# A two-layer encoder's opening: the small columns' load moved behind the modulation weights, and one modulation sum moved to GpSimd

## The chip, the cores and the metric

The kernel runs on one core of a Trainium2 chip. The metric is the device time of one execution in microseconds (us), taken as the median of several runs. A profiled execution has a span (first to last instruction) and a time of its own, a little longer.

## The reference, cut to what matters

Each of two layers modulates its normed input with vectors that come out of a matrix product with one row, `silu(c) @ adaln_w`. The first layer's first two vectors, shift (`v` = 0) and scale (`v` = 1), are needed before any product of the layer can be finished.

```python
mod = jnp.einsum('bd,lde->lbe', jax.nn.silu(c), adaln_w) + adaln_b[:, None, :]
...
    sh1, sc1, g1, sh2, sc2, g2 = jnp.split(mod[layer][:, None, :].astype(x.dtype), 6, axis=-1)
    h = rmsnorm(x, norm_w[layer, 0]) * (1.0 + sc1) + sh1
    y = hybrid_mixer(h, ...)          # proj = h @ w_in, then three branches
...
    x = x + g1 * rmsnorm(y, norm_w[layer, 1])
    h = rmsnorm(x, norm_w[layer, 2]) * (1.0 + sc2) + sh2
    y = swiglu(h, ...) if layer % 2 == 0 else moe_swiglu(h, ...)
    x = x + g2 * rmsnorm(y, norm_w[layer, 3])
```

There are 256 tokens of width 1024, all in float32.

## The kernel before

Every product is made with weights that are split into a rounded high part (`H`, by ScalarE, L319) and a rest (`L`, by VectorE, L320), and the activations likewise into `xH` and `xL`; three matmuls replace one. Weights arrive as tiles of 128 x 1024 float32, 512 KB each, on the DMA queue that SyncE issues (SP). They stand in one list, `plan`; `load_ahead` issues the load of the next entries, `issue_one` splits the next entry, and `take` hands it to the matmuls. Four `raw` buffers hold loaded weights in turn. A load into a buffer waits until the split of its last user is done. SP issues in order, and each load also waits for the load that stands eight places ahead of it in the queue.

The change lies in `begin`, the opening of layer 0, in which TensorE, VectorE and ScalarE run in the order in which the code is written. A modulation vector has 1024 columns in two halves of 512; half 0 serves the first four 128-blocks of the model width, half 1 the last four. For each half and each of the two vectors, four tiles `rawe` (256 of the 1024 rows each, 512 KB) are loaded, and `adaln_add` multiplies them by the column `scol` and sums them into `acc` on VectorE, two instructions a tile (L450 first, then L452). TensorE then sums over the partitions with one-column matmuls (`ad`, L492), in `end`; `bias` adds `adaln_b`. Some tiles go to TensorE straight away instead (the flag `pe`).

With half 0 done, the first halves of `xH` and `xL` exist, and TensorE can multiply with rows 0 to 511 of the weights: `gv` (two tiles, rows 0 to 511, products `pn`), the small columns (48 columns of `w_in`, loaded by two DMAs of many short rows, L814 and L815, products `pg`) and `nk` (two tiles, products `pt`). With half 1 done, the rows 512 to 1023 follow: `gv` from its other two tiles, the rest of the small columns, the rest of `nk`. From there on the list of weights goes on (`nq`, `nv`, ...), and the order is the same before and after.

`gv` is planned first, then the small columns, then `nk`; a permutation of the first seven entries (in `plan_mixer`) sets the order of their loads. `between` is called after each of the first eight modulation tiles, and spreads the loads of `x` and of small rows and the first norm over them. `G` is GpSimd, `V` VectorE, `S` ScalarE.

Of the kernel before, what the change touches and what calls it, by code (L numbers as in the profile page):

```python
# [77 lines left out]
def _build(ctx, tc, nc, A, out, dbg, upto):  # L78
# [121 lines left out]
    def other_loads():  # L200

        nc.sync.dma_start(cc[:, P:], A["consts"][:, P:])
        nc.sync.dma_start(posi, A["positions"].rearrange("b (t p) -> p (b t)", p=P))
        nc.sync.dma_start(gdnA.rearrange("p l e -> p (l e)"), ap(A["gdn_A_log"], 0, [[0, P], [1, 16]]))
        nc.sync.dma_start(gdnB.rearrange("p l e -> p (l e)"), ap(A["gdn_dt_bias"], 0, [[0, P], [1, 16]]))
# [141 lines left out]
    def issue_one(lows=None):  # L347
        nm_, k0, load, early = plan.popleft()
        r = loaded.popleft() if loaded else load()
        ready.append((nm_, k0) + split(r, early, lows) + (early,))  # L350
# [8 lines left out]
    def load_ahead(tags):  # L359

        for tag in tags:
            t = tl("raw1", [P, 1024], tag) if tag else None
            ahead.append(t)
            loaded.append(plan[len(loaded)][2](t))
# [14 lines left out]
    def take(name, ahead=True):  # L379
        if ahead or not any(r[0] == name for r in ready):  # L380
            issue(ahead, name)
        r = next(r for r in ready if r[0] == name)
        ready.remove(r)
        _, k0, H, L, _ = r
        return [(k0 + i, H[:, i, :], L[:, i, :]) for i in range(H.shape[1])]
# [10 lines left out]
    def mm_nat(o, k, H, L, xs, tb, last, parts=(0, 1)):  # L396

        xH, xL = xs
        if 0 in parts:
            mm(o, xH[:, tb, k, :], H, start=k == 0, stop=False)  # L400
            mm(o, xH[:, tb, k, :], L, start=False, stop=False)  # L401
        if 1 in parts:
            mm(o, xL[:, tb, k, :], H, start=False, stop=k == last)  # L403
# [38 lines left out]
        return o if rows < KD else [t.rearrange("p c t n -> p c (t n)") for t in o]  # L442


    def adaln_add(r, k0, acc, first=0):

        for j in range(r.shape[1]):
            k = k0 + j
            if k == first:
                ts(acc, r[:, j, :], scol[:, k:k + 1], None, op0=OP.mult)  # L450
            else:
                stt(acc, r[:, j, :], scol[:, k:k + 1], acc, op0=OP.mult, op1=OP.add)  # L452

# [32 lines left out]
    def sums(half):  # L486

        o = ps("ad", [P, 2, 4])
        accs, begun = {}, []

        def into(v, j, r, c, last):
            mm(o[:, v, j:j + 1], r[:, j * P:j * P + P], c, start=not begun, stop=last, skip_group_check=True)  # L492
            begun.append(1)

        def add(v, k0, r, pe):
            if pe:
                for k in range(2):
                    for j in range(4):
                        into(v, j, r[:, k], scol[:, k0 + k:k0 + k + 1], False)
            else:  # L500
                first = None
                if v not in accs:
                    accs[v], first = tl("acc", [P, 512], ("la2", "m2")[v]), k0
                adaln_add(r, k0, accs[v], first)

        def end(v=None):
            for u in list(accs) if v is None else [v]:
                acc = accs.pop(u)
                for j in range(4):
                    into(u, j, acc, one_c, v is None and j == 3 and not accs)  # L510

        def bias():
            h = slice(half * 4, half * 4 + 4)
            tt(modT[:, 0, 0:2, h], o, adb[:, 0, 0:2, h], op=OP.add)

        return Steps(add=add, end=end, bias=bias)

    def begin(xs, n, part):


        load = lambda v, half, k0: adaln_load(0, v, half, k0, tl("rawe", [P, 1024], "l4"))
        s0 = sums(0)
        for i in range(8):
            v, k0 = (1, 0)[i % 2], i // 2 * 2
            s0.add(v, k0, load(v, 0, k0), i in (1, 3))
            part(i)
        load_ahead([None] * 2)
        order = [(1, 0), (1, 2), (1, 4), (1, 6), (0, 0), (0, 2), (0, 4), (0, 6)]
        late = [load(v, 1, k0) for v, k0 in order[:2]]
        load_ahead([None, None, "l4"])  # L530
        late += [load(v, 1, k0) for v, k0 in order[2:]]
        lows = []
        s0.end()
        issue_one()
        issue_one(lows)
        s0.bias()
        n.scale(slice(0, 4))
        n.hf(0, 0)
        n.hi(0, 0)
        n.lo(0, 0)  # L540
        lows.pop()()
        n.hf(1, 0, 0)
        n.hi(1, 0)
        n.lo(1, 0)
        load_ahead([None] * 2)
        o = [ps("pn", [P, 512], "pw") for _ in range(2)]

        def product(early, tb, i):
            for k, H, L in early:
                mm_nat(o[tb], k, H, L, xs, tb, KD - 1, (i,))  # L550

        s1 = sums(1)
        late = [(v, k0, r, i == 0) for i, ((v, k0), r) in enumerate(zip(order, late))]
        s1.add(*late[0])
        early = [p for _ in range(2) for p in take("gv", False)]
        for tb in range(2):
            for i in range(2):
                product(early, tb, i)
        issue_one()
        s1.add(*late[1])  # L560
        small = take("small", False)
        osm = gates_small(xs, small[:4])
        issue_one()
        load_ahead([None] * 2)
        other_loads()
        s1.add(*late[2])
        issue_one()
        s1.add(*late[3])
        s1.end(1)
        n.tr(0, 1, ("pg",))  # L570
        n.tr(1, 1, ("pl",))
        onk = proj_T("nk", 512, xs, rows=2)
        for i in range(4, 8):
            s1.add(*late[i])
        issue_one(lows)
        issue_one(lows)
        s1.end()
        proj_T("nk", 512, xs, 1, onk, 2, 4)
        lows.pop(0)()
        s1.bias()  # L580
        n.scale(slice(4, 8))
        n.hf(0, 1, 4)
        n.hf(1, 1, 0)
        n.hi(0, 1)
        lows.pop()()
        n.lo(0, 1)
        early = [p for _ in range(2) for p in take("gv", False)]
        n.hi(1, 1)
        n.lo(1, 1)
        for tb in range(2):  # L590
            for i in range(2):
                product(early, tb, i)
        return o, osm, small[4:], onk

    def row_of(col, name):

# [221 lines left out]
    def gates_small(xs, some=None, o=None):  # L818

        xH, xL = xs  # L820
        o = o or ps("pg", [P, 2, P], "pg" if some else "pl")
        for k, H, L in some or take("small"):
            mm(o[:80], H, xH[:, :, k, :], start=k == 0, stop=False)
            mm(o[:80], L, xH[:, :, k, :], start=False, stop=False)
            mm(o[:80], H, xL[:, :, k, :], start=False, stop=k == KD - 1)
        if k < KD - 1:
            return o
        pump()

        wd = tl("wd", [80, T], "l1")  # L830
        S.copy(wd, o[:80].rearrange("p t n -> p (t n)"))
        G.memset(wd[32:33], 1.0)
        return wd
# [500 lines left out]
    def plan_mixer(l):  # L1334
        w = A["w_in"][l]
        for b in BLOCKS:
            if b == "small":
                plan.append((b, 0, lambda t=None: load_small(w, t), "g4" if l == 0 else None))
            elif b == "out":
                add(b, lambda k0, kn: kview(A["w_out"][l], 0, D, k0, kn), KD, D,  # L1340
                    spare=None if l else "l4")
            elif b[0] == "b":
                n, hf = int(b[1]), int(b[2])
                add(b, lambda k0, kn, n=n, hf=hf: kview(A["w_branch"][l, n], hf * 512, 512, k0, kn), 4, 512)
            else:
                c0 = COL["mg"] + int(b[2]) * D + int(b[3]) * 512 if b[:2] == "mg" else COL[b]
                add(b, lambda k0, kn, c0=c0: kview(w, c0, 512, k0, kn), KD, 512, 4 if b == "gv" else 0, back=6)
        if l == 0:

            first = [plan.popleft() for _ in range(7)]  # L1350
            plan.extendleft(reversed([first[i] for i in (0, 1, 4, 5, 6, 2, 3)]))

    def mixer(l, xs, o, more, then=(), begun=(None, None, None)):
        v = tl("gv", [P, 2, 512], "l4")
# [677 lines left out]

    def between(i):
        n = norm[1]
        for j in ((2,), (3,), (0,), (1, 4, 5, 6), (), (7,), (), ())[i]:
            load_rows(j)
        if i in (0, 1):
            for h in range(2):
                n.sq(i, h)
        elif i == 2:  # L2040
            n.rs(0)
            n.rs(1)
        elif i in (3, 4):
            n.xn(i - 3, 0)
        elif i in (5, 6):
            n.tr(i - 5, 0, ("pg", "pw"))
            columns(i - 5)

    def params():
        columns(2)  # L2050
# [59 lines left out]
```

## Time and profile before

| | |
|---|---|
| median of 3 runs | 1883.06 us (1881.93 to 1888.7) |
| profiled execution, its own time | 1880.3 us |
| its span | 1878.5 us |
| TensorE busy (share of the span) | 1825.1 us (97%) |
| VectorE busy | 1593.7 us (85%) |
| ScalarE busy | 1320.0 us (70%) |
| GpSimd busy | 28.0 us (1%) |
| HBM read | 528.02 MB, 282 GB/s over the span |

Times in the text are microseconds from the span's start. The change moves instructions in the first 60 us or so of 1878.5. Busy time of TensorE counts a matmul until its modelled end, so a busy TensorE can still run at half rate; the distance between the starts of two matmuls tells that.

### The profile page before, as it was taken

How to read it: one execution, taken by the hardware profiler on the slowest of the kernel's cores; microseconds unless marked ns; L12 is line 12 of the kernel's file. 1: busy time of each engine (PE TensorE's matmuls, PEld its weight loads, DVE VectorE, ACT ScalarE, POOL GpSimd, SP SyncE). 2: the span in 40 equal slices, each digit the busy share in tenths (PEclk: the TensorE clock that was granted, in tenths of full speed). 3: DMA queues.
4: the chain of work that ended last, by engine and by line, in shares of the span. 5: the costliest groups of instructions: out<-in, count | busy, mean ns of one | idle time of the engine just before them, and what ended most of it. 6: DMA issues, size and time to landing. Idle time of an engine off the chain costs nothing.

```text
span 1878.5 us, 33240 instructions
## 1 busy us (share of the span) xinstructions
PE 1825.1 (97%) x11984; PEld 1538.5 (82%) x11984; DVE 1593.7 (85%) x2034; ACT 1320.0 (70%) x1872; POOL 28.0 (1%) x54
## 2 busy tenths in 40 slices
PE   7999999999989999999999999999999999999997
PEld 6987888799878977788788888888888888878785
DVE  6887977777766887877798998999989999999998
ACT  3786476643445783576688788787887888888885
POOL 0000000000000000000000000000000000000000
PEclk9999999999999999999999999999999999999998
DMA  9545766478883546758899999999999999999993
GB/s 318 164 143 159 226 191 191 150 250 265 274 278 114 161 140 191 227 161 318 274 364 315 344 349 344 360 374 369 367 336 364 379 368 379 391 385 394 393 392 150
DMA packets 258026, 531.35 MB, mean 283 GB/s; under 512 B 22126, under 2 KB 45116, under 8 KB 257852
## 3 DMA queue, kind: packets, MB, share of 16 engines
q1 hardware_dynamic: 257500, 528.99, 81.1%
q8 instruction: 96, 1.57, 0.4%
q14 instruction: 78, 0.64, 0.1%
q0 software_dynamic: 192, 0.07, 0.0%
q10 hardware_dynamic: 160, 0.07, 0.0%
HBM read 528.02 MB, written 1.05 MB: 282 GB/s over the span
## 4 chain that ended last, share of the span: by engine, by line
PE 72%; DVE 10%; DMA 9%; ACT 5%; issue 3%; POOL 0%; SPq 0%; DVEq 0%; ACTq 0%; POOLq 0%
PE mo L1974 10%; PE mo L1973 10%; PE mo L1975 10%; DVE wl L320 5%; DMA raw<-in_adaln_w 4%; PE pn L400 4%; PE pn L403 3%; PE my L1898 3%; PE my L1899 3%; PE my L1900 3%; PE pn L401 3%; DMA raw<-in_ffn_w 2%; ACT wh L319 2%; PE pt L439 2%; PE pt L440 2%
## 5 line engine op out<-in xcount | busy, mean ns | idle before, releaser
L320 DVE TENSOR_TENSOR wl<-raw,wh 128x1024 fp32r<-128x1024 f32 (+1 forms) x893 | 1067.5, 1221 | 141.0 <-ACT wh L319 110.1
L319 ACT CAST wh<-raw 128x1024 fp32r<-128x1024 f32 (+1 forms) x893 | 927.4, 1054 | 339.9 <-DMA raw<-in_ffn_w 79.1
L1973 PE MATMUL mo<-wh,gx 128*128 128x512 f32 x896 | 356.3, 398 | 0.1
L1974 PE MATMUL mo<-wl,gx 128*128 128x512 f32 x896 | 351.0, 392 | 2.0 <-DVE wl L320 1.9
L1975 PE MATMUL mo<-wh,gx 128*128 128x512 f32 x896 | 350.4, 391 | 0.0
L1974 PEld LDWEIGHTS mo<-wl,gx 128*128 128x128 f32 x896 | 168.8, 188 | 38.9 <-DVE wl L320 5.5
L1975 PEld LDWEIGHTS mo<-wh,gx 128*128 128x128 f32 x896 | 168.5, 188 | 35.8 <-ACT gx L1869 0.4
L1973 PEld LDWEIGHTS mo<-wh,gx 128*128 128x128 f32 x896 | 168.7, 188 | 32.7 <-ACT gx L1869 0.5
L440 PE MATMUL pt<-xH,wl 128*128 128x256 f32 x576 | 164.0, 285 | 3.5 <-DVE wl L320 3.5
L439 PE MATMUL pt<-xH,wh 128*128 128x256 f32 x576 | 166.3, 289 | 0.5 <-ACT wh L319 0.5
L441 PE MATMUL pt<-xL,wh 128*128 128x256 f32 x576 | 163.6, 284 | 0.0
L400 PE MATMUL pn<-wh,xH 128*128 128x512 f32 x352 | 148.6, 422 | 0.0
L403 PE MATMUL pn<-wh,xL 128*128 128x512 f32 x352 | 138.6, 394 | 0.0
L401 PE MATMUL pn<-wl,xH 128*128 128x512 f32 x352 | 138.5, 393 | 0.0
L452 DVE SCALAR_TENSOR_TENSOR acc<-raw,scol,acc 128x512 f32<-128x512 f32 x140 | 104.7, 748 | 28.8 <-DMA raw<-in_adaln_w 27.2
L440 PEld LDWEIGHTS pt<-xH,wl 128*128 128x128 f32 x576 | 111.0, 193 | 4.6 <-DVE wl L320 4.3
L439 PEld LDWEIGHTS pt<-xH,wh 128*128 128x128 f32 x576 | 110.9, 193 | 1.0 <-ACT wh L319 0.7
L441 PEld LDWEIGHTS pt<-xL,wh 128*128 128x128 f32 x576 | 111.0, 193 | 0.0
L1898 PE MATMUL my<-wh,aTm 128*128 128x512 f32 x280 | 109.1, 390 | 0.0
L1899 PE MATMUL my<-wl,aTm 128*128 128x512 f32 x280 | 109.0, 389 | 0.0
L1900 PE MATMUL my<-wh,aTm 128*128 128x512 f32 x280 | 108.9, 389 | 0.0
L400 PEld LDWEIGHTS pn<-wh,xH 128*128 128x128 f32 x352 | 66.5, 189 | 19.0 <-issue 7.4
(474 smaller groups left out, 2605.2 us busy)
## 6 DMA issues: line engine op xcount, KB each, us to landing
raw<-in_moe_w SPq DMA_DIRECT2D x672, 512.0 KB, 5.8
raw<-in_w_in SPq DMA_DIRECT2D x128, 512.0 KB, 3.9
raw<-in_adaln_w SPq DMA_DIRECT2D x80, 512.0 KB, 4.7
raw<-in_ffn_w SPq DMA_DIRECT2D x66, 512.0 KB, 4.7
raw<-in_w_branch SPq DMA_DIRECT2D x24, 512.0 KB, 4.3
rawe<-in_adaln_w SPq DMA_DIRECT2D x16, 512.0 KB, 7.9
raw<-in_w_out SPq DMA_DIRECT2D x16, 512.0 KB, 4.7
x<-in_x SPq DMA_DIRECT2D x2, 512.0 KB, 6.9
```

Source lines behind the costliest of these rows:

```text
L319: S.copy(H, r)
L320: low = lambda: tt(L, r, H, op=OP.subtract)
L400: mm(o, xH[:, tb, k, :], H, start=k == 0, stop=False)
L401: mm(o, xH[:, tb, k, :], L, start=False, stop=False)
L403: mm(o, xL[:, tb, k, :], H, start=False, stop=k == last)
L439: mm(d, H[:, cs], xH[:, :, k, :], start=k == 0 and c % 2 == 0, stop=False, skip_group_check=True)
L440: mm(d, L[:, cs], xH[:, :, k, :], start=False, stop=False, skip_group_check=True)
L441: mm(d, H[:, cs], xL[:, :, k, :], start=False, stop=k == KD - 1, skip_group_check=True)
L1898: mm(y[hf], aT[:, 0, k, :], H[:, c], start=first, stop=False)
L1973: mm(q, gH[:, k, :], H, start=k == 0, stop=False)
L1974: mm(q, gH[:, k, :], L, start=False, stop=False)
L1975: mm(q, gL[:, k, :], H, start=False, stop=k == KD - 1)
```

## The change

The second halves' eight tiles are all loaded right behind the first two `gv` tiles, alternating between the vectors. The small columns' load goes behind the other `gv` tiles, and all of the small columns' product moves behind `gv`'s. The scale vector's second half is summed on GpSimd (a multiply in place and an add, where VectorE has one instruction), the shift vector's on VectorE, none on TensorE. Of the first `gv` products, the second token block's is made behind the second halves' sums. Two extra matmuls (`keep_warm`) stand around the end of the first sums. `between` loads the second block of `x` three places later.

```diff
-    def adaln_add(r, k0, acc, first=0):
+    def adaln_add(r, k0, acc, first=0, eng=V):
...
             if k == first:
-                ts(acc, r[:, j, :], scol[:, k:k + 1], None, op0=OP.mult)
+                eng.tensor_scalar(acc, r[:, j, :], scol[:, k:k + 1], None, op0=OP.mult)
+            elif eng is G:
+                G.tensor_scalar(r[:, j, :], r[:, j, :], scol[:, k:k + 1], None, op0=OP.mult)
+                G.tensor_tensor(acc, r[:, j, :], acc, op=OP.add)
             else:
                 stt(acc, r[:, j, :], scol[:, k:k + 1], acc, op0=OP.mult, op1=OP.add)
...
-                adaln_add(r, k0, accs[v], first)
+                adaln_add(r, k0, accs[v], first, G if v == half == 1 else V)
...
+    def keep_warm():
+
+        mm(ps("warm", [P, 512], "pw"), ident, x[:, 0, 0:512], start=True, stop=True)
...
         load_ahead([None] * 2)
-        order = [(1, 0), (1, 2), (1, 4), (1, 6), (0, 0), (0, 2), (0, 4), (0, 6)]
-        late = [load(v, 1, k0) for v, k0 in order[:2]]
-        load_ahead([None, None, "l4"])
-        late += [load(v, 1, k0) for v, k0 in order[2:]]
+        order = [(v, k0) for k0 in range(0, KD, 2) for v in (1, 0)]
+        late = [(v, k0, load(v, 1, k0), False) for v, k0 in order]
+        load_ahead([None] * 2)
         lows = []
+        keep_warm()
         s0.end()
+        keep_warm()
...
         s1 = sums(1)
-        late = [(v, k0, r, i == 0) for i, ((v, k0), r) in enumerate(zip(order, late))]
-        s1.add(*late[0])
+        for p in late[0::2]:
+            s1.add(*p)
         early = [p for _ in range(2) for p in take("gv", False)]
-        for tb in range(2):
-            for i in range(2):
-                product(early, tb, i)
+        product(early, 0)
         issue_one()
         s1.add(*late[1])
-        small = take("small", False)
-        osm = gates_small(xs, small[:4])
-        issue_one()
-        load_ahead([None] * 2)
-        other_loads()
-        s1.add(*late[2])
-        issue_one()
+        issue_one(lows)
+        lows.pop()()
+        load_ahead([None])
         s1.add(*late[3])
-        s1.end(1)
         n.tr(0, 1, ("pg",))
         n.tr(1, 1, ("pl",))
         onk = proj_T("nk", 512, xs, rows=2)
-        for i in range(4, 8):
-            s1.add(*late[i])
+        s1.add(*late[5])
+        s1.add(*late[7])
+        other_loads()
         issue_one(lows)
         issue_one(lows)
+        proj_T("nk", 512, xs, 1, onk, 2, 4)
         s1.end()
-        proj_T("nk", 512, xs, 1, onk, 2, 4)
+        product(early, 1)
         lows.pop(0)()
         s1.bias()
...
-        return o, osm, small[4:], onk
+            product(early, tb)
+        return o, None, None, onk
...
-            plan.extendleft(reversed([first[i] for i in (0, 1, 4, 5, 6, 2, 3)]))
+            plan.extendleft(reversed([first[i] for i in (0, 1, 5, 6, 2, 3, 4)]))
...
-        for j in ((2,), (3,), (0,), (1, 4, 5, 6), (), (7,), (), ())[i]:
+        for j in ((2,), (0,), (1, 4), (3, 5, 6), (), (), (), (7,))[i]:
```

Three places show how the queues change. In the rows, a number behind a name is a tile's own. First the DMA queue (SP) from the second half's first tile on; `rawe_215` to `rawe_237` are the second halves' tiles, `raw_219` the small columns, `raw_223` and `raw_1_225` the first two `nk` tiles, `raw_269` the third `gv` tile. Before:

```order
L286 DMA rawe_217<-in_adaln_w 128x2x512
L814 DMA raw_219<-in_w_in 128x8x32
L815 DMA raw_219<-in_w_in 128x8x16
L286 DMA raw_223<-in_w_in 128x2x512
L286 DMA raw_1_225<-in_w_in 128x2x512
L286 DMA rawe_227<-in_adaln_w 128x2x512
...
L286 DMA rawe_237<-in_adaln_w 128x2x512
L286 DMA raw_269<-in_w_in 128x2x512
```

In the changed kernel the first `nk` tiles are `raw_231` and `raw_233`, the third and fourth `gv` tiles `raw_269` and `raw_271`, the small columns `raw_315`:

```order
L286 DMA rawe_217<-in_adaln_w 128x2x512
...
L286 DMA rawe_229<-in_adaln_w 128x2x512
L286 DMA raw_231<-in_w_in 128x2x512
L286 DMA raw_233<-in_w_in 128x2x512
L286 DMA raw_269<-in_w_in 128x2x512
L286 DMA raw_271<-in_w_in 128x2x512
L817 DMA raw_315<-in_w_in 128x8x32
L818 DMA raw_315<-in_w_in 128x8x16
```

The small columns moved from in front of six modulation tiles to behind four weight tiles, and the `nk` tiles from in front of those six to behind them.

Second, VectorE from the end of the first activations' split (`xL`) to the second halves' bias (`modT`). Before:

```order
L661 TENSOR_TENSOR xL_107<-hf_178,xH_106 128x512
L320 TENSOR_TENSOR we_309<-raw_219,we_308 128x640
L450 TENSOR_SCALAR acc_312<-rawe_217,scol 128x512
L452 SCALAR_TENSOR_TENSOR acc_312<-rawe_217,scol,acc_312 128x512
L320 TENSOR_TENSOR wl_329<-raw_223,wh_328 128x1024
...
L450 TENSOR_SCALAR acc_388<-rawe_231,scol 128x512
...
L452 SCALAR_TENSOR_TENSOR acc_388<-rawe_237,scol,acc_388 128x512 x2
L320 TENSOR_TENSOR we_398<-raw_269,we_397 128x1024
L514 TENSOR_TENSOR modT<-ad_275,abT 128x2x4
```

And in the changed kernel:

```order
L664 TENSOR_TENSOR xL_107<-hf_178,xH_106 128x512
L320 TENSOR_TENSOR wl_305<-raw_231,wh_304 128x1024
L450 TENSOR_SCALAR acc_308<-rawe_217,scol 128x512
L455 SCALAR_TENSOR_TENSOR acc_308<-rawe_217,scol,acc_308 128x512
L320 TENSOR_TENSOR wl_312<-raw_233,wh_311 128x1024
L455 SCALAR_TENSOR_TENSOR acc_308<-rawe_221,scol,acc_308 128x512 x2
L455 SCALAR_TENSOR_TENSOR acc_308<-rawe_225,scol,acc_308 128x512 x2
L455 SCALAR_TENSOR_TENSOR acc_308<-rawe_229,scol,acc_308 128x512 x2
L320 TENSOR_TENSOR we_366<-raw_269,we_365 128x1024
L517 TENSOR_TENSOR modT<-ad_275,abT 128x2x4
```

VectorE has 8 summing instructions of the second halves instead of 14, and all of them now stand behind the split of the first `nk` tile.

Third, TensorE around the end of the second halves' sums (`ad`): `pt` is `nk`'s product, `pn_274` that of `gv`'s second token block, `pg` that of the small columns. In the changed kernel:

```order
L441 MATMUL pt_332<-xL_107,wh_311 128x256
L495 MATMUL ad_275<-kon,acc_276 128x1 x4
L495 MATMUL ad_275<-kon,acc_308 128x1 x4
L400 MATMUL pn_274<-we_247,xH_106 128x512
...
L403 MATMUL pn_274<-we_251,xL_107 128x512 x2
L400 MATMUL pn_273<-we_365,xH_106 128x512
```

Before, the 12 matmuls of `pn_274` stood ahead of all `nk` products, and the last 24 matmuls of `pt` between `ad_275` and the third `gv` tile.

## Rows read from the trace of the kernel before

**Rows 1.** The DMA's share and rate by stretch.

```profile
core 0: us, , PEclk, DMA share, GB/s
0.00:24.00 24.00, 1.00 0.93 319
24.00:32.00 8.00, 1.00 0.77 202
32.00:46.00 14.00, 1.00 1.05 389
```

**Rows 2.** SP's DMA issues in order of time: start, duration, line, transfer.

```profile
16.56 0.59 SPq L814 DMA_DIRECT2D raw<-in_w_in  x1
17.19 5.45 SPq L815 DMA_DIRECT2D raw<-in_w_in  x1
22.68 3.60 SPq L286 DMA_DIRECT2D raw<-in_w_in  x2
26.38 4.72 SPq L286 DMA_DIRECT2D rawe<-in_adaln_w  x6
```

**Rows 3.** VectorE's timeline: start, duration, line, operation, what its idle time ended with.

```profile
35.24 1.22 DVE L320 TENSOR_TENSOR wl<-raw,wh 128x1024 fp32r<-128x1024 f32 x1
36.58 1.54 DVE L452 SCALAR_TENSOR_TENSOR acc<-rawe,scol,acc 128x512 f32<-128x512 f32 x2
38.03 0.48 DVE L450 TENSOR_SCALAR acc<-rawe,scol 128x512 f32<-128x512 f32 x1
38.55 5.48 DVE L452 SCALAR_TENSOR_TENSOR acc<-rawe,scol,acc 128x512 f32<-128x512 f32 x7
45.49 0.16 DVE L514 TENSOR_TENSOR modT<-ad,abT 128x8 f32<-128x8 f32 x1
```

**Rows 4.** The chain that ended last, in order of time, TensorE's pieces.

```profile
44.08 1.05 PE ad L492 x8
45.60 0.12 PE pt L439
48.71 0.21 PE pt L439
49.35 0.43 PE pn L400
53.80 0.23 PE pn L400
56.69 0.15 PE pt L439
```

**Rows 5.** TensorE's busy time, granted clock and DMA by stretch.

```profile
28.00:33.00 5.00, 5.00 (x14) 1.00 1.02 308
37.30:45.00 7.70, 5.97 (x51) 1.00 1.05 390
46.40:49.20 2.80, 2.80 (x16) 0.50 0.93 244
55.20:60.00 4.80, 4.80 (x42) 1.00 0.27 69
```

**Rows 6.** ScalarE's timeline.

```profile
23.30 1.04 ACT L319 CAST we<-raw 128x1024 fp32r<-128x1024 f32 x1 [0.98 <-DMA raw<-in_w_in]
43.27 1.05 ACT L319 CAST we<-raw 128x1024 fp32r<-128x1024 f32 x1 [9.84 <-DMA raw<-in_w_in]
47.33 1.15 ACT L657 CAST xH<-hf 128x512 fp32r<-128x512 f32 x2
```

**Rows 7.** TensorE's timeline: the first second-half tile.

```profile
24.80 3.54 PE L492 MATMUL ad<-scol,rawe 128*128 128x1 f32 x16 [1.15 <-DMA rawe<-in_adaln_w]
```

**Rows 8.** GpSimd's and VectorE's timelines, two copies and what ran beside one.

```profile
136.60 0.81 POOL L995 COPY Yc<-cc 128x256 f32<-128x256 f32 x1
221.15 0.45 POOL L995 COPY Yc<-cc 128x256 f32<-128x256 f32 x1 [83.74 <-DVE Yf L1040]
...
136.47 0.69 DVE L1176 TENSOR_TENSOR d<-bT 128x512 f32<-128x512 f32 x1
137.07 0.88 DVE L1177 TENSOR_TENSOR d<-bT 128x512 f32<-128x512 f32 x1
...
138.48 0.68 DVE L1177 TENSOR_TENSOR d<-bT 128x512 f32<-128x512 f32 x1
```

More of the change, by code (lines that the diff above doesn't have):

```diff
@@ L546, in begin, with product @@
         o = [ps("pn", [P, 512], "pw") for _ in range(2)]
-        def product(early, tb, i):
-            for k, H, L in early:
-                mm_nat(o[tb], k, H, L, xs, tb, KD - 1, (i,))
+        def product(early, tb):
+            for i in range(2):
+                for k, H, L in early:
+                    mm_nat(o[tb], k, H, L, xs, tb, KD - 1, (i,))
         s1 = sums(1)
-        late = [(v, k0, r, i == 0) for i, ((v, k0), r) in enumerate(zip(order, late))]
-        s1.add(*late[0])
+        for p in late[0::2]:
+            s1.add(*p)
         early = [p for _ in range(2) for p in take("gv", False)]
-        for tb in range(2):
-            for i in range(2):
-                product(early, tb, i)
+        product(early, 0)
         issue_one()
         s1.add(*late[1])
-        small = take("small", False)
-        osm = gates_small(xs, small[:4])
-        issue_one()
-        load_ahead([None] * 2)
-        other_loads()
-        s1.add(*late[2])
-        issue_one()
+        issue_one(lows)
+        lows.pop()()
+        load_ahead([None])
         s1.add(*late[3])
-        s1.end(1)
         n.tr(0, 1, ("pg",))
@@ L590, in begin @@
         for tb in range(2):
-            for i in range(2):
-                product(early, tb, i)
-        return o, osm, small[4:], onk
+            product(early, tb)
+        return o, None, None, onk
     def row_of(col, name):
@@ L2034, in between @@
         n = norm[1]
-        for j in ((2,), (3,), (0,), (1, 4, 5, 6), (), (7,), (), ())[i]:
+        for j in ((2,), (0,), (1, 4), (3, 5, 6), (), (), (), (7,))[i]:
             load_rows(j)
-        if i in (0, 1):
+        if i in (0, 3):
             for h in range(2):
-                n.sq(i, h)
+                n.sq(i // 3, h)
         elif i == 2:
             n.rs(0)
+            n.xn(0, 0)
+        elif i == 4:
             n.rs(1)
[L2043 to L2047, printed above, removed]
+            n.xn(1, 0)
+            n.tr(0, 0, ("pg", "pw"))
+            columns(0)
+        elif i == 6:
+            n.tr(1, 0, ("pg", "pw"))
+            columns(1)
     def params():
```

## The prediction

> **What bounds the kernel now.** Over the whole span TensorE bounds it (97% busy), and from 56.69, where it takes up the fifth row block of `nk`, its work is the same before and after [rows 4]. So the change is worth what it does to that one moment. I read the chain in order of time first, then the stretch before 56.69 engine by engine, then the DMA. The chain [rows 4] reaches 56.69 over matmuls alone from 44.08 on; what starts them there are the sums of the second halves on VectorE: from 36.58 to 44.03 it sums without a gap [rows 3], and TensorE is busy in only 5.97 of the 7.70 us from 37.30 to 45.00 [rows 5]. VectorE is that late because the tiles are late. The DMA moves 319 GB/s up to 24 and 389 from 32 to 46, but 202 in between [rows 1]; there the queue stands behind the small columns' second load, whose issue alone takes 5.45 us, and the six modulation tiles are issued only from 26.38 [rows 2]. That hole is worth (389 − 202) × 8 us = 1.5 MB, 3.8 us at the full rate.
>
> **The change, step by step.** The question is when TensorE reaches the same matmul.
>
> *The DMA.* Up to the first two `gv` tiles the queue carries the same bytes, so I take the same 319 × 24 = 7.66 MB by 24.0. What VectorE needs next is no longer a modulation tile but `nk`'s first tile, since that split now stands ahead of its sums; it is the 21st transfer of 0.524 MB, with 0.15 MB of small rows 11.15 MB in all. At 389 GB/s the 3.50 MB left arrive by 33.0. That is the early bound. The late one comes from the third `gv` tile before: 23 transfers, 0.34 MB of small ones, 12.40 MB. By 32 there were 9.27 MB, so by rate it was due at 40.0; its cast waited for it until 43.27 [rows 1, 6], 3.2 us late, because transfers in flight share the engines. With that delay `nk` lands at 36.2. Behind the third `gv` tile 2.2 MB were queued, behind `nk`'s first tile now 1.57 MB: 1.57/2.2 of 3.2 is 2.3, so I take 35.3.
>
> *VectorE.* Six summing instructions leave it, but the rest begins later. Cast 1.05 [rows 6]: 36.4. Split 1.22 [rows 3]: 37.6. The first shift tile, 0.52 + 0.78 by the starts in [rows 3]: 38.9. Split of the second `nk` tile: 40.1. Six more sums at 5.48/7 = 0.78: **44.8**, against 44.03 before. The gain of the earlier tiles is waited away in front of the `nk` split.
>
> *TensorE.* The first product of `gv` no longer has the 3.54 us of one-column matmuls ahead of it [rows 7] and may begin two us earlier; nothing comes of it, since the next thing is `nk`, and TensorE waits for it from about 31 to 37.6. Behind a wait it runs slowly: in 28 to 33 it makes 14 recorded matmuls in 5 us, and in 46.40 to 49.20 the granted clock is 0.50, the lower of its two levels [rows 5], with 0.21 between starts instead of 0.12 [rows 4]. `nk`'s 48 matmuls then take 5 us at 0.21 (24) and 24 × 0.12 = 2.9: done at 45.5, a little behind VectorE. The column sums (`ad`) take 1.05 [rows 4]: 46.6, and the bias comes 0.36 later as before (45.49 − 45.13) [rows 3, 4]: **46.9**, 1.5 us later than 45.49. From the bias to the first `xH` it took 1.84 + 0.6 [rows 3, 6]; TensorE fills this with the 12 matmuls of `pn_274`, 12 × 0.23 = 2.8 [rows 4]. Then 24 more `gv` matmuls, 5.6, to 55.0. Last the small columns: 24 matmuls of the same 256 columns at 0.12, 2.8, where 12 stood here before. With 0.1 for what else stands there, `nk` goes on at 57.9: **+1.2 us**.
>
> *GpSimd.* It gets 8 multiplies and 7 additions of 128x512. No such row exists. A copy of 256 elements takes 0.45 by itself and 0.81 beside a two-input VectorE instruction [rows 8]. A multiply therefore costs 0.45 to 1.6, an addition with two inputs 0.45 to 3.2; alone and doubled for size the copy gives at most 0.90, and I take 0.7 and 1.1, 13.3 us in all. The first scale tile is there at about 24.8 [rows 7], the last about two transfers ahead of `nk`'s, near 33; its four instructions take 3.6, so the sum is done by 38 to 40, before TensorE asks for it at 45.5. It costs nothing then, except through VectorE. The same rows show a cost there: beside the copy, VectorE's L1177 took 0.88 instead of 0.68. A multiply of 512 would cost 0.4, an addition 0.8. Two or three of GpSimd's instructions are left when VectorE gets going at 36.4: about 1.6 us, of which 0.7 vanish in the 0.7 that VectorE is ahead of TensorE; with the chance that GpSimd is done by then I count **+0.4**.
>
> *Costed at nothing.* The two warming matmuls stand where TensorE waits, for VectorE's first sums and then for the first `xH`; uncovered each costs the 0.43 of a 512-column matmul at the low rate [rows 4]. The second block of `x` comes a few us later, while ScalarE waits for the second `gv` tile until 23.30 [rows 6]; a later block would delay the first `xH`, behind which TensorE has six free us. The small columns' two loads now stand ahead of the constants and of `nk`'s third tile. They can be issued when the first `nk` split frees their buffer at 37.6; with 4 us of queue they are there by 44 and are needed at 55. `nk`'s third tile is issued behind them at about 45, needed at 57.9; the DMA has room, 69 GB/s in 55 to 60 [rows 5].
>
> *Sum.* 1880.3 + 1.2 + 0.4 = 1881.9 for an execution like the profiled one. The median of the runs shown lies 2.8 above it, so **1884.7**.
>
> **The rivals.** The measurement can tell about 0.5%, 9.4 us, from no change.
>
> *A, as above* (0.64): 1882 to 1887. The uncertain landing of `nk` (33.0 to 36.2) and 2 us for VectorE's collisions make this range.
>
> *B, GpSimd's sum ends last* (0.13). TensorE stands in order at `ad` until GpSimd is done, with everything of the layer queued behind it. It decides from a mean of (45.5 − 24.8)/15 = 1.4 us an instruction on. For it: 1.6 and more are within the bounds, and nearly every instruction waits for the one before it. Against it: the copy alone takes 0.45. At 2.0 the sum ends at 54.8, 9.3 us late: 1893.9, slower by more than 0.5%. At the upper bounds (35 us) it is 14 late.
>
> *C, GpSimd and VectorE hold each other up all along* (0.13). If one's instruction fully excludes the other's, GpSimd is already behind when VectorE starts, and the rest of it alternates with VectorE's ten instructions: with 3 multiplies and 4 additions left, 3 × 0.4 + 4 × 0.8 = 4.4, less the 0.7: +3.7, 1888.0. For it: copy and VectorE's instruction both grew when they met [rows 8]. The Trainium skill speaks for this: SBUF — State Buffer, section "SBUF: two separate sides", calls the port pair of the two engines an exclusive lock, which a VectorE instruction with two SBUF inputs takes too. The trace agrees as far as it goes, with 0.88 against 0.68 [rows 8]; by the skill's rule the time would be C's, by a lighter reading of these rows A's. Against it: VectorE waits from about 29 to 36, and GpSimd has that time by itself.
>
> *D, the hole in the DMA is what counted* (0.10). `nk` lands at 33.0, GpSimd is done in time, and `nk` runs at full rate: VectorE is done at 42.5, `ad` at 43.0, 3.6 earlier than in A: −2.4 us, 1880.7. For it: the hole of 3.8 us is gone. Against it: tiles have landed 3 us behind the rate, and VectorE has 7.5 us to do behind the `nk` tile's arrival, whatever came earlier.
>
> **How the numbers follow.** The time is A's, 1884.7. The range takes in D, with a little over 1 us that the median of the runs moves by itself, and C and the milder half of B: 1879.5 to 1891. Faster by over 0.5% would need `nk` to go on at 47, before the sums can be there by any of these numbers: 0.02. Slower by over 0.5% is B at 2.0 us an instruction and more: 0.06. The rest, 0.92, is within 0.5%.
>
> **What would show it.** In the changed profile: no stretch at 202 GB/s before 32; VectorE idle from about 29 until ScalarE's cast of `nk`'s first tile, at 35 to 36; GpSimd's last addition by 40; the bias at about 47 (45.49 before) and `nk`'s fifth block at about 58 (56.69). It is wrong if TensorE waits for GpSimd at `ad`, if the tile lands much before 34, or if the fifth block of `nk` or the small columns are themselves late and open a wait after 55.

## The result and the profile after

The changed kernel is slower: 1893.67 us (median of 8 runs, 1888.12 to 1904.53) beside 1881.72 for the kernel before on the same chip, a ratio of 1.0065 with an interval of [1.0041, 1.0088]. The prediction was 1884.7 with a range up to 1891. The profiled execution took 1888.6 us (span 1886.8); before it was 1880.3.

GpSimd's timeline in the changed kernel (start, duration, line, operation; in brackets its idle time and what ended it):

```profile
22.26 1.57 POOL L450 TENSOR_SCALAR acc<-rawe,scol 128x512 f32<-128x512 f32 x1 [6.03 <-DMA rawe<-in_adaln_w]
23.82 1.55 POOL L452 TENSOR_SCALAR rawe<-rawe,scol 128x512 f32<-128x512 f32 x1
25.45 2.00 POOL L453 TENSOR_TENSOR acc<-rawe,acc 128x512 f32<-128x512 f32 x1
27.43 3.54 POOL L452 TENSOR_SCALAR rawe<-rawe,scol 128x512 f32<-128x512 f32 x2
30.94 2.60 POOL L453 TENSOR_TENSOR acc<-rawe,acc 128x512 f32<-128x512 f32 x2
33.51 3.19 POOL L452 TENSOR_SCALAR rawe<-rawe,scol 128x512 f32<-128x512 f32 x2
36.68 3.58 POOL L453 TENSOR_TENSOR acc<-rawe,acc 128x512 f32<-128x512 f32 x2
40.24 3.88 POOL L452 TENSOR_SCALAR rawe<-rawe,scol 128x512 f32<-128x512 f32 x2
44.09 3.27 POOL L453 TENSOR_TENSOR acc<-rawe,acc 128x512 f32<-128x512 f32 x2
```

The 15 instructions stand without a gap from 22.26 to 47.36: 25.1 us, 1.67 each. While VectorE is idle, from 28.0 to 34.0, a multiply takes 1.55 and an addition 1.30 (the mean of the two at 30.94); beside VectorE single ones take up to 2.00 and 2.14. That sum is what TensorE waits for:

```profile
34.04 0.49 PE L439 MATMUL pt<-xH,wh 128*128 128x256 f32 x1 [4.32 <-ACT wh L319]
47.42 3.23 PE L495 MATMUL ad<-kon,acc 128*128 128x1 f32 x16 [3.72 <-POOL acc L453]
```

VectorE in the same stretch, to be held against [rows 3]:

```profile
34.02 1.25 DVE L320 TENSOR_TENSOR wl<-raw,wh 128x1024 fp32r<-128x1024 f32 x1 [6.03 <-ACT wh L319]
35.20 0.91 DVE L450 TENSOR_SCALAR acc<-rawe,scol 128x512 f32<-128x512 f32 x1
36.14 0.75 DVE L455 SCALAR_TENSOR_TENSOR acc<-rawe,scol,acc 128x512 f32<-128x512 f32 x1
36.81 2.31 DVE L320 TENSOR_TENSOR wl<-raw,wh 128x1024 fp32r<-128x1024 f32 x1
39.05 7.20 DVE L455 SCALAR_TENSOR_TENSOR acc<-rawe,scol,acc 128x512 f32<-128x512 f32 x6
50.69 0.17 DVE L517 TENSOR_TENSOR modT<-ad,abT 128x8 f32<-128x8 f32 x1 [2.24 <-PE ad L495]
```

It is slowed too: a split took 2.31 instead of 1.22, a sum 7.20/6 = 1.20 instead of 0.78. Its own sums end at 46.25, 1.1 before GpSimd's.

ScalarE's cast of `nk`'s first tile, and the stretches of the DMA and of the granted clock (columns: stretch, its length, busy time of PE, PEld, DVE, ACT, POOL, then the granted clock, the DMA's share, GB/s):

```profile
32.95 1.04 ACT L319 CAST wh<-raw 128x1024 fp32r<-128x1024 f32 x1 [6.44 <-DMA raw<-in_w_in]
```

```profile
24.00:32.00 8.00, 5.22 (x20) 4.09 (x20) 3.29 (x3) 2.47 (x6) 7.92 (x5) 0.79 1.04 387
32.00:46.00 14.00, 8.85 (x48) 8.36 (x48) 11.76 (x10) 4.18 (x4) 13.77 (x10) 0.76 0.74 230
46.00:50.00 4.00, 2.58 (x14) 2.58 (x14) 2.44 (x2) 0.00 (x0) 4.00 (x6) 0.73 0.12 14
50.00:55.00 5.00, 5.00 (x15) 4.08 (x15) 4.24 (x10) 3.85 (x8) 0.81 (x2) 0.53 0.47 115
```

The hole of 202 GB/s [rows 1] is gone, 387 in its place, and the tile is there at 32.95. The gain is waited away: in 46 to 50 the DMA moves 14 GB/s, and the granted clock from 50 to 55 is 0.53, most of it at the lower of its two levels. The chain that ended last, in order of time, reads the same way, from the tile over GpSimd to TensorE:

```profile
13.25 8.84 DMA rawe<-in_adaln_w
...
45.77 1.60 POOL acc L453
47.42 3.23 PE ad L495 x16
50.65 0.64 PE pn L400
...
54.27 1.16 PE pn L403 x4
55.43 0.23 PE pn L400
...
63.91 0.15 PE pt L439
```

The last row answers to 56.69 in [rows 4]: the opening costs 7.2 us.

### The profile page after: what moved, and what is told of

It reads as the page before. It is cut to its first block, busy times and chain, and to the rows that moved or that the text cites. A ratio compares the mean times of both kernels' runs of the same rounds, so it can differ in the third digit from the quotient of the medians.

```text
span 1886.8 us, 33229 instructions
## 1 busy us (share of the span) xinstructions
PE 1829.3 (97%) x11972; PEld 1539.9 (82%) x11972; DVE 1595.3 (85%) x2028; ACT 1320.5 (70%) x1872; POOL 53.5 (3%) x69
## 3 DMA queue, kind: packets, MB, share of 16 engines
q8 instruction: 96, 1.57, 0.3%
HBM read 528.02 MB, written 1.05 MB: 280 GB/s over the span
## 4 chain that ended last, share of the span: by engine, by line
PE 79%; DMA 8%; DVE 6%; ACT 2%; issue 2%; POOL 1%; ACTq 0%; SPq 0%; DVEq 0%; POOLq 0%
PE mo L1977 10%; PE mo L1976 10%; PE mo L1978 10%; PE pn L400 5%; PE pn L403 5%; PE pn L401 5%; PE my L1901 3%; PE my L1902 3%; PE my L1903 3%; DVE wl L320 3%; DMA raw<-in_ffn_w 3%; PE pt L439 2%; PE pt L440 2%; PE pt L441 2%; DMA raw<-in_adaln_w 2%
## 5 line engine op out<-in xcount | busy, mean ns | idle before, releaser
L400 PEld LDWEIGHTS pn<-wh,xH 128*128 128x128 f32 x352 | 67.2, 191 | 19.5 <-issue 7.7
```

## The experiments

All times are medians, with the ratio to the kernel before on the same chip, whose median was 1883.2 to 1883.8 us. "Opening" is how much later, in us, the first matmul of `nk`'s fifth block starts than in the kernel before (56.47 in the timeline).

| kernel | us | ratio, interval | opening |
|---|---|---|---|
| both sums on VectorE | 1883.19 | 1.0001 [0.9986, 1.0015] | -0.6 |
| the same again | 1885.34 | 1.0008 [0.9998, 1.0017] | 0.0 |
| changed, the wait filled | 1892.03 | 1.0041 [1.0026, 1.0055] | +6.1 |
| changed, half of the sum on GpSimd | 1892.60 | 1.0043 [1.0029, 1.0057] | +5.2 |
| changed, GpSimd multiplies two tensors | 1892.36 | 1.0053 [1.0036, 1.0071] | +5.4 |
| changed again | 1896.18 | 1.0066 [1.0049, 1.0083] | +8.3 |
| VectorE, small columns first | 1889.88 | 1.0033 [1.0018, 1.0047] | +1.7 |
| VectorE, early wait filled | 1891.90 | 1.0048 [1.0034, 1.0063] | +1.6 |
| VectorE, twelve matmuls more | 1890.01 | 1.0032 [1.0014, 1.0051] | -0.7 |
| the same again | 1888.42 | 1.0021 [1.0009, 1.0033] | -0.4 |
| changed, twelve matmuls more | 1894.09 | 1.0053 [1.0040, 1.0066] | +8.9 |
| VectorE, no warming matmuls | 1886.29 | 1.0008 [0.9998, 1.0019] | +0.4 |

**Both sums on VectorE.** Everything of the change but GpSimd's part.

```diff
-                adaln_add(r, k0, accs[v], first, G if v == half == 1 else V)
+                adaln_add(r, k0, accs[v], first, V)
```

> The changed kernel with the scale vector's second half summed on VectorE (16 instructions at 0.77 us, 8 of them where it waits for the first nk tile) and all else as in the changed kernel. Theory T (GpSimd's sum ends last: 15 instructions at 1.67 us, TensorE stands 3.7 us in front of it and then runs slowly): the column sums start when nk's first 48 matmuls end, at 43 to 44 instead of 47.4, the fifth nk block at about 56 instead of 63.9, and the time falls 7 to 12 us below the changed kernel, to within 3 us of before. Theory R (the new order of loads and products costs the time, whoever sums): the fifth nk block stays past 61 and the time at least 5 us above before.

Measured: no difference to the kernel before, twice (the second time on another chip). VectorE sums the scale tiles in its wait, from 28.48 to 34.47; the splits and the other sums then take 8.1 us, from 34.39 to 42.52, where the changed kernel needs 12.2 (34.02 to 46.25). TensorE comes from `nk` to `ad` at 42.88 without a wait:

```profile
29.00 5.47 DVE L455 SCALAR_TENSOR_TENSOR acc<-rawe,scol,acc 128x512 f32<-128x512 f32 x7
37.84 4.68 DVE L455 SCALAR_TENSOR_TENSOR acc<-rawe,scol,acc 128x512 f32<-128x512 f32 x6
42.88 1.84 PE L495 MATMUL ad<-kon,acc 128*128 128x1 f32 x16
```

So the loss is GpSimd's sum, and the new order by itself is worth half a microsecond at most in the opening.

> The kernel with both sums on VectorE once more, on the same chip as the next. Theory S: 1883 to 1887, and within 2 us of the next. Rival R (the twelve small matmuls of the next one cost something far behind): it is 5 us or more faster than the next, as in the runs on two chips.

It was 1885.34. The changed kernel ran on this chip too, at 1896.18 (below): 10.8 us between the two medians, 8.3 of which the openings show.

**The wait filled.** Four 128x512 matmuls with no reader stand ahead of `ad` in the changed kernel.

```diff
+        for _ in range(4):
+            mm(o[1], ident, x[:, 0, 0:512], start=True, stop=True)
         s1.end()
         product(early, 1)
```

> The changed kernel with four more 128x512 float32 matmuls into a bank that is overwritten later, on TensorE ahead of the column sums, where it stands idle from 43.7 to 47.4. If part of the loss is the low clock after the wait: the column sums take about 1.1 instead of 3.2 us and the 12 gv matmuls behind them start 0.23 apart instead of 0.43, the fifth nk block comes at about 60 instead of 63.9 and the time falls by about 4 us. If the loss is the wait alone: the fifth nk block stays within 0.7 us of 63.9. Theory R gives no change either.

TensorE's wait falls to 1.27 us and `ad` to 1.95 from 3.23, with the clock granted in full in 46 to 50 where it was 0.73:

```profile
47.91 1.95 PE L495 MATMUL ad<-kon,acc 128*128 128x1 f32 x16 [1.27 <-POOL acc L453]
```

But `ad` still begins when GpSimd is done, and the opening gains 1.1 of 7.2. The low clock behind the wait is a part of the price, and the smaller one: against the kernel with both sums on VectorE, `ad` begins 4.5 later in the changed kernel (47.42 instead of 42.88), and from there to the fifth block it is 16.3 instead of 13.0. Filling the wait gives back 1.6 of these 3.3 (14.7), since the twelve products behind `ad` still take 4.3 (49.72 to 54.01).

**Half of the sum on GpSimd.** Two of the four scale tiles go to VectorE, behind its own.

```diff
-adaln_add(r, k0, accs[v], first, G if v == half == 1 else V)
+adaln_add(r, k0, accs[v], first, G if v == half == 1 and k0 < 4 else V)
...
-        for p in late[0::2]:
+        for p in late[0:4:2]:
...
         s1.add(*late[7])
+        s1.add(*late[4])
+        s1.add(*late[6])
```

> The changed kernel with the scale vector's first two late tiles on GpSimd (7 instructions) and the other two on VectorE behind its own sums. Theory T: GpSimd is done near 34, before TensorE asks; VectorE ends last at about 45.5, TensorE waits about 1.8 us, the fifth nk block at about 58 to 59, the time 1 to 3 us above before. If GpSimd hurts by holding VectorE up, not by its own end: VectorE ends at 48 or later and the fifth nk block past 61. Theory R: past 61 as well.

GpSimd is done at 33.9, before VectorE goes on, and VectorE's splits and sums are at full speed again, ten sums in 7.85:

```profile
37.53 7.85 DVE L455 SCALAR_TENSOR_TENSOR acc<-rawe,scol,acc 128x512 f32<-128x512 f32 x10
```

```profile
45.44 3.32 PE L495 MATMUL ad<-kon,acc 128*128 128x1 f32 x16 [2.69 <-DVE acc L455]
```

Now VectorE is what TensorE waits for, with four sums that it could have done for nothing in its wait. Only 2 us of the 7.2 come back, less than theory T has (the fifth block at 61.7, not 58 to 59; the median 1.0043, some 8 us above before, not 1 to 3). Theory T left out the clock: behind this wait of 2.69, too, it is 16.3 from `ad` to the fifth block.

**GpSimd multiplies two tensors.** The column of scalars is given as a tensor, broadcast along the row.

```diff
-G.tensor_scalar(r[:, j, :], r[:, j, :], scol[:, k:k + 1], None, op0=OP.mult)
+G.tensor_tensor(r[:, j, :], r[:, j, :], scol[:, k:k + 1].to_broadcast([P, 512]), op=OP.mult)
```

(and the same for the first multiply)

> The changed kernel with GpSimd's eight multiplications written as a product of two tensors (the column broadcast along the row) instead of a tensor by a column of scalars. GpSimd took 1.55 to 1.77 us for the multiplication by scalars and 1.3 us for an addition of two tensors while VectorE was idle. Theory G1 (GpSimd's price is that of 512 elements in each of 128 lanes, whatever the form): GpSimd's work ends at 46 to 48 us, bias at 50 to 51, time within 1 us of the changed kernel's. Rival G2 (the form with scalars is the dear one): a multiplication costs as an addition, 1.3 us; eight save some 3 us, the work ends at about 44, the opening ends 3 us earlier than the changed kernel's. Rival G3 (a third operand is one more read, and the form is dearer): ends at 50 or later.

GpSimd's first rows, then VectorE's and TensorE's:

```profile
22.55 1.04 POOL L451 TENSOR_TENSOR acc<-rawe,scol 128x512 f32<-128x512 f32 x1 [6.02 <-DMA rawe<-in_adaln_w]
23.55 1.03 POOL L455 TENSOR_TENSOR rawe<-rawe,scol 128x512 f32<-128x512 f32 x1
24.67 1.27 POOL L456 TENSOR_TENSOR acc<-rawe,acc 128x512 f32<-128x512 f32 x1
```

```profile
29.38 1.77 DVE L667 TENSOR_TENSOR xL<-hf,xH 128x512 fp32r<-128x512 f32 x1
...
36.52 1.50 DVE L453 TENSOR_SCALAR acc<-rawe,scol 128x512 f32<-128x512 f32 x1
38.05 1.41 DVE L458 SCALAR_TENSOR_TENSOR acc<-rawe,scol,acc 128x512 f32<-128x512 f32 x1
```

```profile
48.06 1.25 PE L498 MATMUL ad<-kon,acc 128*128 128x1 f32 x8 [2.40 <-DVE acc L458]
```

The form with scalars is the dear one: 1.55 against 1.04. GpSimd's sum ends at 44.28, 3 us earlier, as G2 has it. But the opening gains 1.8, not 3: VectorE is held up more, its sums end at 48.0, and TensorE waits for VectorE. The first multiply of its sum took 1.50 instead of 0.48, but beside GpSimd's additions (34.24 to 37.73), which the changed kernel has as well; beside the new multiplies (37.70 to 40.36) a sum took 1.41, where beside the old ones it took 0.75 to 1.06.

**Small columns first.** Their load stands again behind the second of the late tiles, with both sums on VectorE.

```diff
-        late = [(v, k0, load(v, 1, k0), False) for v, k0 in order]
+        late = [(v, k0, load(v, 1, k0), False) for v, k0 in order[:2]]
+        small = plan[6]
+        t = tl("raw1", [P, 1024], "l4")
+        sm = small[2](t)
...
+        late += [(v, k0, load(v, 1, k0), False) for v, k0 in order[2:]]
```

> The kernel of the run with both sums on VectorE, with the small columns' transfer put back between the second and the third of the late tiles, in a tile of its own. It prices the one thing that the reordered loads are to bring. In the profile before, the small columns' stretch moved 202 GB/s in 24 to 32 us where the changed kernel moved 387. Theory T (the transfers' order is worth about 2 us): the first tile of nk is cast at about 35 to 35.6 us instead of 33.2 of the run with both sums on VectorE, the opening ends 1.5 to 2.4 us later than there, and the whole is 1884.5 to 1886. Rival (the slow stretch is filled by other queues, so the order is worth nothing): cast at 33 to 33.6, time 1883 to 1883.5.

`nk`'s first tile is cast at 35.70 instead of 33.17 with both sums on VectorE, and the opening ends 2.2 us later than there. So the order of the transfers is worth what theory T says in the opening. The median lost more than theory T has, 0.33% against the kernel before (1889.88, not 1884.5 to 1886); what lies behind the opening is taken up below.

**The early wait filled.** Both sums off GpSimd; TensorE takes two of the eight tiles and VectorE four ahead of the `nk` splits, with extra matmuls between.

```diff
+        for p in late[2:6]:
+            s1.add(*p)
...
+        for v, k0, r, _ in late[:2]:
+            warm_o(o[1])
+            s1.add(v, k0, r, True)
+        warm_o(o[1])
```

> No sum on GpSimd; two late tiles on TensorE as one-column matmuls in its idle time before the nk tile, with three warming matmuls; four late tiles on VectorE ahead of the nk splits, the last two behind them. If what is left of the cost is VectorE waiting in front of the nk split and TensorE's low clock behind its own wait: VectorE is done by 40, nk's 48 matmuls start 0.12 apart, the column sums start at 41 to 43, the fifth nk block comes at 53.5 to 55.5 (56.7 before), and the time is 1 to 3 us below before. If the gain of the earlier tiles is lost somewhere else: no better than before.

TensorE takes 1.84 for each of its tiles and, with the extra matmuls between, begins `nk` at 37.55 instead of 34.27. `ad` begins at 45.04 instead of 42.88, and now VectorE, done early, waits 4.97 us for it. The fifth block comes at 58.0, not at 53.5 to 55.5: TensorE had taken over work that VectorE can hide.

**Twelve small matmuls more.** These runs are about a second loss, behind the opening. At one place near 172 us nine profiles with the changed order show a wait that the kernel before doesn't have. TensorE's timeline of the changed kernel, of the kernel before, and of the kernel with twelve matmuls more:

```profile
178.66 0.97 PE L1257 MATMUL lo<-gs,bT 64*64 64x128 f32 x21
182.16 0.43 PE L1257 MATMUL lo<-gs,bT 64*64 64x128 f32 x3 [2.52 <-issue]
```

```profile
171.18 1.17 PE L1254 MATMUL lo<-gs,bT 64*64 64x128 f32 x24
176.91 1.16 PE L1249 MATMUL lo<-gv,am 128*128 128x128 f32 x8 [1.57 <-DVE y_gla L805]
```

```profile
170.40 1.09 PE L1260 MATMUL lo<-gs,bT 64*64 64x128 f32 x24
176.66 1.16 PE L1255 MATMUL lo<-gv,am 128*128 128x128 f32 x8 [2.22 <-DVE y_gla L811]
```

In the first the 24 matmuls break off after 21 and wait 2.5 us for nothing that the profile shows (`issue`).

```diff
         keep_warm()
+        pad = ps("warm", [P, 512], "pw")
+        for _ in range(12):
+            mm(pad[:, 0:8], ident, x[:, 0, 0:8], start=True, stop=True)
         issue_one()
```

> The kernel with both sums on VectorE and twelve small matmuls (128x8) more in TensorE's wait at 24 us, whose results nobody reads: they shift every later TensorE instruction by twelve in its program. The changed kernel and the runs with both sums on VectorE, with the filled wait and with half of the sum on GpSimd all show one stall of TensorE of 1.5 to 2.9 us at the 64x64 products behind the 128 small q products near 172 us, put down to issue, with one packet of the instruction queue in it; the kernel before, with six matmuls more ahead of it, and the run with the early wait filled, with nineteen more, have none there. Theory P (the stall hangs on where in TensorE's instruction stream that place falls): no issue stall over 0.5 us between 160 and 190 us, and the place behind it within 0.3 us of before's shift in the opening; the time is 0.5 to 1.5 us under that of the run with both sums on VectorE, since what follows there waits for VectorE anyway. Rival Q (it comes from the moment at which the bulk transfers stand there): the stall of 1.5 to 2.9 us is still there.

> The changed kernel, with GpSimd's sum, and the same twelve small matmuls. Theory P: the stall of 2.5 us near 180 us is gone, the shift against the kernel before stays 7.2 to 7.5 us up to 190 us, and the time is 1 to 2.5 us under the changed kernel's. Rival Q: stall and time as in the changed kernel. In both, the low clock of the stretch near 240 us may remain, since its cause is the wait ahead of it.

> The twelve small matmuls with both sums on VectorE once more. By the profile it loses 0.7 us less in the opening and no stall near 172 us, and its median was yet 6.4 us over the kernel before. Theory S: 1883 to 1887 here, within 2 us of the kernel without the twelve. Rival R: 1889 to 1891.

All three profiles with the twelve matmuls have no such wait there; all nine profiles of the changed order without them or other added work of that size have it, 1.5 to 2.9 us. The break moves with the stream: with four matmuls more (eight rows of the trace), in the run with the wait filled, it falls after 13 of the 24; without the two warming matmuls it falls behind all 24, two products further on. The kernel with the early wait filled, nineteen matmuls longer at that place than the changed one, and the kernel before, six longer, have none. So the place in TensorE's instruction stream decides, as far as these runs tell, and theory P holds for the stall. It doesn't hold for the time: the next products wait for VectorE's `y_gla` anyway (1.57 to 2.4 us). On VectorE the medians are worse, 1890.01 and 1888.42; on one chip the twelve cost 3.1 us, more than theory S's 2 and less than rival R's 5. With GpSimd the ratio is 1.0053, within the interval of the changed kernel's, and the opening is +8.9, not the 7.2 to 7.5 that P has.

**No warming matmuls.** `keep_warm` taken out, both sums on VectorE.

```diff
-        keep_warm()
         s0.end()
-        keep_warm()
```

> The kernel with both sums on VectorE without the two 128x512 matmuls on either side of the first column sums, whose results nobody reads. They stand where TensorE waits. Theory N (they cost nothing and give nothing): ad of the second halves begins at 42.9 us as with them, give or take 0.5, the granted clock of the stretch 24 to 32 is lower than 0.79, and the time is within 1.5 us of the kernel with them. Rival K (they keep the clock up for the gv products): the matmuls of the first gv products from 25.8 on come at 0.43 us from each other in either, but those of nk from 35 on stay at 0.21 for longer, and the opening ends 1 us or more later.

`ad` begins at 43.85, 0.4 later than with them on the same chip (43.47), and the two have the same ratio, 1.0008: they are worth nothing that can be measured in the time. The clock that theory N names for 24 to 32 can't be read: the column gives 1.00 there while the first `gv` products start 0.43 apart.

**The changed kernel again.**

> The changed kernel once more, on the chip of the next three, with a second profile. The opening must cost again 7 to 7.5 us at the fifth block of nk, GpSimd's sum 25 us. Theory S (what is lost behind the opening are single stretches at the lower clock that come and go between executions): other places than in the first profile of it have the lower clock behind 66 us (there near 253, 386, 724 and 796 us), while the stall at the 64x64 products near 180 us is there again; median 1890 to 1895. Rival R (the loss behind the opening is the program's): the same four places, the same shift of 10 to 11 us at 281 us.

The opening is +8.3, the stall is there with 2.60 us, the median 1896.18, a little above theory S's 1895. (The places that the expectation names are counted from some 8 to 10 us ahead of the span's start.) Of the changed kernel's four places with the lower clock behind the opening (near 244, 376, 716 and 788) the first and the third came again; two others, near 775 and 933, took the place of the rest. The kernel before has such places too, near 710 and 918, so those near 716 and 933 are not the change's own. The changed kernel's windows, then this run's (stretch, length, busy time of TensorE, granted clock, DMA share, GB/s):

```profile
240.00:265.00 25.00, 24.88 (x229) 0.93 0.58 182
...
935.00:955.00 20.00, 20.00 (x93) 1.00 0.91 310
```

```profile
240.00:265.00 25.00, 23.67 (x225) 0.86 0.61 191
...
935.00:955.00 20.00, 19.97 (x91) 0.88 0.76 234
```

## Why the prediction was wrong

**The step that failed is GpSimd's price**: "I take 0.7 and 1.1, 13.3 us in all", done "by 38 to 40". It was 25.1 us, done at 47.36. By themselves the two lie inside the bounds (0.45 to 1.6 and 0.45 to 3.2; measured 1.55 and 1.30), but the choice inside them was wrong, and beside VectorE the multiply passed its bound (1.72 on average over the eight; the additions 1.64): I scaled a copy by its size [rows 8], and a multiply by a column of scalars cost 3.4 times that copy, not 1.6 times. What came is rival B, by its own rule: it decides from 1.4 us an instruction, and the mean was 1.67. At 1.55 and 1.30 throughout, the 15 would have taken 21.5 and been done at 43.8, just when TensorE was ready (43.7); the 3.6 more that they took beside VectorE are about the 3.72 that TensorE waited. Its first tile landed 2.5 earlier than the 24.8 I counted from, or the opening would have lost more.

**"+0.4" for VectorE** failed with it. When VectorE got going, at 34.02, GpSimd was on the eighth of its 15 instructions, not on one of the last three, and all of VectorE's work met them: 12.2 us instead of 8.1, **+4.1**. This is rival C, which had +3.7. It can't be added to B: the two end at about the same time, 46.25 and 47.36, and TensorE waits for the later one. In the run with two tensors GpSimd ended 3.1 earlier and VectorE 1.7 later, and VectorE held `ad` up. From 33.51 on, GpSimd's four multiplies and four additions at 1.55 and 1.30 and VectorE's 8.1 would make 19.5 one after the other; both were done in 13.9. The Trainium skill's rule (SBUF — State Buffer, "SBUF: two separate sides", an exclusive lock) gives the direction, but not the size here.

**The clock behind the wait** was in the text for `nk`, not for `ad`. `ad` took 3.23; with the clock kept up 1.84 (both sums on VectorE). The twelve products behind it take 4.8 (50.65 to 55.43) instead of 2.8. So +7.2 goes: `ad` begins 3.3 later than 44.08, takes 2.2 longer than 1.05 (0.8 of it because 16 one-column passes stand there instead of 8), and from its end to the fifth block it is 13.0 instead of 11.3, +1.7. (In 28 to 33 of [rows 5] the clock column reads 1.00 beside `gv` products that start 0.43 apart, as it does ahead of 30 us in some other profiles here; the distance between the starts, by which I took this stretch for slow, is the safer sign.)

**The DMA.** `nk`'s first tile came at 32.95, the early bound (33.0), not at 35.3: the lag of the third `gv` tile [rows 6], which I carried over in part, didn't come back. Here D was right. With both sums on VectorE one sees what D is worth: VectorE done at 42.52 (D: 42.5), but `ad`, which D has done at 43.0, is done at 44.7, since it takes 1.84 (D left it 0.5, less than the 1.05 of its own rows), and the opening gains 0.0 to 0.6, not 2.4.

**Right** were: VectorE's chain behind the tile (8.1 us for the two splits and the eight instructions, 8.4 counted), that the warming matmuls cost nothing, and that neither the small columns nor `nk`'s fifth block are late; TensorE has no wait from 50.51 to the fifth block.

**From the opening to the median.** The time is 9.0 above the forecast. 5.6 of it is the opening (+7.2, not +1.6), 1.1 comes behind it in the profiled execution (+8.3 in all), and 2.3 because the median lies 5.1 above that execution, not 2.8. Only the opening is explained by the steps above.

**What stays open.** The changed kernel is 0.65% slower in both measurements, 9 to 16 us in the second, of which the opening shows 7.2 and 8.3. At about 281 us (a `gup` MEMSET on GpSimd) the shift has grown to +10.7 and +14.6. But with both sums on VectorE it grows too, from -0.6 and 0.0 to +2.0 and +5.9, and these runs' medians are near that of the kernel before, whose profiled execution is 3 us under its median. So most of this part is not GpSimd's. The profiles show two things in it: the stall at issue, of which 1.4 us come back in the next wait, and single stretches at the lower clock, some of which differ between executions. Whether they make up all of it is not shown. Why the kernels on VectorE with the twelve matmuls, with the small columns first and with the early wait filled lose 4 to 9 us by the ratio, with openings of -0.7 to +1.7, is not settled: the mean clock of their runs is lower (0.990 to 0.991 against 0.993 of the kernel before), but it was 0.991 in the second run with both sums on VectorE as well, which lost next to nothing. The profiled executions of these kernels are among their shorter ones, so what the others lose was not seen. No version beat the kernel before.

## What to carry to other kernels

Before an elementwise sum goes to GpSimd, price its own form in a profile: here 128x512 took 1.55 (scalars) and 1.30 (two tensors), against 0.48 and 0.75 in VectorE's one pass. Look for idle time of the faster engine first: VectorE waited 6.0 us in just this stretch, and the same sum took it 6.0. And a sum that ends last costs twice, once for its lateness (4.5 us here) and once for TensorE's clock behind the wait (3.3).

## What the runs showed of the hardware

On GpSimd a multiply by a column of scalars took 1.55 us for 128x512, the same product with the column broadcast as a tensor 1.04, an addition 1.25 to 1.30. GpSimd and VectorE slow each other but overlap in part, and GpSimd's form matters. In the first profile of the changed kernel, beside its multiplies by scalars, VectorE's split took 1.25 (1.22 alone) and its sums 0.75 to 1.06 (0.75 alone); beside its additions a split took 2.31 and sums 1.63 and 1.76. Behind bursts of 128 tiny matmuls TensorE stood up to 2.9 us for nothing that the profile shows, in some alignments of its stream and not in others. A packet of the instruction queue begins within about a microsecond of the gap's start in all nine profiles; that TensorE waits for its instructions there is inferred from it.
